# The first weights on a second DMA queue, and a shorter run of constant products, at the start of a gated hybrid block

## The chip, the cores and the metric

The kernel runs on one core of a Trainium2 chip. The metric is the device time of one execution in microseconds (us): 1506.85 is the median of 3 runs of the kernel before (1506.75 to 1508.6).

The core has five engines with a queue of instructions each: TensorE (PE: matrix products, with the weight loads shown apart as PEld), VectorE (DVE), ScalarE (ACT), GpSimd (POOL) and SyncE (SP). DMA transfers are issued by instructions on an engine's queue, here mostly SP's.

## The reference

The input x has 512 rows (frames) of 2048 channels. With a row norm ahead, it goes through one wide projection, whose columns feed a gated linear recurrence (branch A), a differential attention (branch B) and two merge gates; the branches are projected back, merged and projected out:

```
h    = x * rsqrt(mean(x^2) + eps) * norm_w
proj = h @ w_in                                  # 2048 -> 8*1024 + 2*2048
ya   = hgrn2(a_q, a_f, a_i) * silu(a_g)          # 8 heads of 128, chunks of 64
yb   = diff_attention(b_q, b_k, b_v) * silu(b_g) # 8 heads
out  = x + (sigmoid(gate_a) * (ya @ w_branch_a)
          + sigmoid(gate_b) * (yb @ w_branch_b)) @ w_out
```

The change touches only the start of the first piece of `h @ w_in`.

## The kernel before, in words

All activations are kept transposed, channels on the 128 partitions and the 512 frames along the row; x arrives as 16 tiles of 128x512 (`xT`). Products are made in a split form: each float32 operand is cut into a high part (rounded to the fp32r type) and a low part (the remainder), and high x high, high x low and low x high are summed in PSUM. So every tile of x and every tile of weights needs two conversions before TensorE can use it: a copy on ScalarE for the high part (L134 for x, L182 for weights) and a subtraction on VectorE for the low part (L135, L183).

`gemm` (L164 and on) runs over steps of KC = 2 tiles of 128 channels. In one step it loads the weights of both tiles (128x2x512, `raw`), converts them into `whi` and `wlo`, and issues 4 column blocks x 2 tiles x 3 products, 24 in all, into four PSUM accumulators. Three rings of buffers serve the weights: two raw ones, three high and three low. The conversions stand under a higher priority.

`proj_a(0, True)` is the first gemm: eight steps for the columns of q and f of the first two heads. Since nothing is loaded yet, its function `before` issues the loads of x tile by tile beside those of the weights, all on SP's queue, and calls `load_h`, which makes the high and low parts of x (L134, L135) and the running sum of squares (L138, L140, L141). The first step is converted tile by tile, the later ones as a whole. Its weights come in two pieces per tile, 128x256 each, one for the columns of q and one for those of f. The norm factor of each frame is applied after the product, so `make_rstd` (L143 and on) runs inside the last step.

Ahead of that stand a small load of constants on ScalarE's queue (L97), the tile `ones` (L101), one exponential on ScalarE that brings its table load (L105), and 14 products of `ones` with itself into a PSUM tile that is not read (L109). In the trace each of these float32 products is two passes, so 14 are 28.

The order of instructions on each engine is not the order of the text: the tile framework plans it (`schedule_with_timeline_sim=True`) from priorities, which follow the text, and a simulated timeline. Slots for x and for other 128x512 tiles (`slots`) are handed out first in, first out.

Further on come the other projections and mixers, the gates and the last projection by a scheme with seven half-size products (L677, with conversions L639, L640 and splits L577, L578); the change does not touch them.

Of the kernel before, what the change touches and what calls it, by code (L numbers as in the profile page):

```python
# [11 lines left out]
F32R = mybir.dt.float32r  # L12
# [5 lines left out]
P = 128  # L18
T = 512
NT = T // P  # L20
D = 2048
NK = D // P
WA = 1024
# [6 lines left out]
KC = 2  # L30
# [36 lines left out]
def hybrid_block(ctx: ExitStack, tc: tile.TileContext, xT, w_in, w_a, w_b, w_out,  # L67
                 smalls, cbase, cmask, outT):
    nc = tc.nc
# [14 lines left out]
    slots = Slots(spool, NSLOT)  # L84
    bigs = Slots(bpool, NBIG, "b", (P, 2, T))

    raws, his, los = deque((16, 17)), deque((18, 19, 20)), deque((21, 22, 23))

    def acc_tile():
        return ps_acc.tile([P, T], F32, name="acc", tag="acc")  # L90

    def mix_tile():
        return ps_mix.tile([P, T], F32, name="mix", tag="mix")


    sm = lead.tile([P, LEAD], F32, name="sm")
    nc.scalar.dma_start(out=sm[:, 0:C_LAM], in_=smalls[:, 0:C_LAM])  # L97
    ident = const.tile([P, P], F32, name="ident")
    make_identity(nc, ident)
    ones = const.tile([P, P], F32, name="ones")  # L100
# [4 lines left out]
    nc.scalar.activation(out=warm, in_=ones[:, 0:1], func=AF.Exp)  # L105

    ps0 = mix_tile()
    for i in range(14):
        nc.tensor.matmul(ps0[:, 0:P], lhsT=ones, rhs=ones, start=True, stop=True)  # L109
    masks_s = slots.get(U8, (P, 4, 384))  # L110
    masks = masks_s[0]
# [1 line left out]
    def load_masks():  # L113
        for i in range(4):
            mi = slots.get(mybir.dt.int32)
            nc.sync.dma_start(out=mi[0][:, 0:384], in_=cmask[:, i, :])
            nc.gpsimd.tensor_copy(out=masks[:, i, :], in_=mi[0][:, 0:384])
            slots.put(mi)
# [11 lines left out]
    def load_h(k, xs):  # L130
        sq = slots.get()
        x_t = xs[0]
        nw = sm[:, C_NW + k:C_NW + k + 1]
        nc.scalar.activation(out=h_hi[k], in_=x_t, func=AF.Copy, scale=nw)  # L134
        nc.vector.scalar_tensor_tensor(out=h_lo[k], in0=x_t, scalar=nw, in1=h_hi[k].bitcast(F32),  # L135
                                       op0=MUL, op1=SUB)
        if k == 0:
            nc.scalar.activation(out=xacc, in_=x_t, func=AF.Square)  # L138
        else:
            nc.scalar.activation(out=sq[0], in_=x_t, func=AF.Square)  # L140
            nc.vector.tensor_tensor(out=xacc, in0=xacc, in1=sq[0], op=ADD)  # L141
        slots.put(xs, sq)
# [21 lines left out]
    def gemm(wsrc, nk, a_hi, a_lo, stationary_w, evac, before=None, after=None, done=None, turn_at=1):  # L164
        accs = [acc_tile() for _ in range(4)]
        nb = nk // KC
        for kb in range(nb):
            if kb == turn_at:
                while later:
                    later.pop(0)()  # L170
            three = [bigs.get(ring=raws), bigs.get(F32R, ring=his), bigs.get(F32R, ring=los)]
            raw, whi, wlo = (t for t, _ in three)
            if before is not None:
                before(kb, wsrc(raw, kb))
            else:
                for dst, src in wsrc(raw, kb):
                    nc.sync.dma_start(out=dst, in_=src)
            with tc.high_priority(offset=PRIO):
                step = 1 if before is not None and kb == 0 else KC
                for c in range(0, KC, step):  # L180
                    cs = slice(c, c + step)
                    nc.scalar.activation(out=whi[:, cs, :], in_=raw[:, cs, :], func=AF.Copy)  # L182
                    nc.vector.tensor_tensor(out=wlo[:, cs, :], in0=raw[:, cs, :], in1=whi[:, cs, :].bitcast(F32),  # L183
                                            op=SUB)
            if after is not None and kb == nb - 1:
                with tc.high_priority(offset=PRIO):
                    after()
            for j in range(4):
                for c in range(KC):
                    k = kb * KC + c  # L190
                    js = slice(j * P, (j + 1) * P)
                    if stationary_w:
                        prods = ((whi[:, c, js], a_hi[k]), (whi[:, c, js], a_lo[k]), (wlo[:, c, js], a_hi[k]))
                    else:
                        prods = ((a_hi[k][:, js], whi[:, c, :]), (a_hi[k][:, js], wlo[:, c, :]),
                                 (a_lo[k][:, js], whi[:, c, :]))
                    for n, (l, r) in enumerate(prods):
                        nc.tensor.matmul(accs[j], lhsT=l, rhs=r, start=(k == 0 and n == 0),  # L198
                                         stop=(k == nk - 1 and n == 2))
                if kb == nb - 1:  # L200
                    with tc.high_priority(offset=PRIO):
                        evac(j, accs[j])
            for ring, (_, i) in zip((raws, his, los), three):
                ring.append(i)
            recent[:] = [whi[:, 0, :]]
            if done is not None:
                done(kb)
# [7 lines left out]
    def two_cols(w, c0, c1):  # L215
        def src(raw, kb):
            r = []
            for i, c in enumerate((c0, c1)):
                rows = w[kb * KC * P:(kb + 1) * KC * P, c:c + T // 2].rearrange("(c p) n -> p c n", p=P)
                r.append((raw[:, :, i * (T // 2):(i + 1) * (T // 2)], rows))  # L220
            return r
        return src


    def evac_rows(tiles):
        def evac(j, acc):
            s = slots.get()
            nc.scalar.activation(out=s[0], in_=acc, func=AF.Copy, scale=rstd_t[:, j:j + 1])
            tiles.append(s)
        return evac  # L230


    def evac_cols(tiles):
        def evac(j, acc):
            s = slots.get()
            nc.vector.tensor_tensor(out=s[0], in0=acc, in1=rstdB, op=MUL)
            tiles.append(s)
        return evac

    def silu(aps):  # L240
        n = aps[0].shape[1]
        sg = [slots.get() for _ in aps]
        for a, g in zip(aps, sg):
            nc.scalar.activation(out=g[0][:, 0:n], in_=a, func=AF.Sigmoid)
        for a, g in zip(aps, sg):
            nc.vector.tensor_tensor(out=a, in0=a, in1=g[0][:, 0:n], op=MUL)
        slots.put(*sg)
# [162 lines left out]
    def proj_a(p, first):  # L410
        c = p * 256
        qz, vg = [], []
        before = after = None
        if first:
            xs = [slots.get() for _ in range(NK)]

            def load_x(k):
                nc.sync.dma_start(out=xs[k][0], in_=xT[k * P:(k + 1) * P, :])

            def before(kb, wsrc):  # L420

                for k in range(3 * kb - 1, min(3 * kb + 2, NK)) if kb else ():
                    load_x(k)
                for c in range(KC):
                    k = kb * KC + c
                    if kb == 0:
                        load_x(c)
                    for dst, src in wsrc:
                        nc.sync.dma_start(out=dst[:, c], in_=src[:, c])
                    load_h(k, xs[k])  # L430
            after = make_rstd
        gemm(two_cols(w_in, c, WA + c), NK, h_hi, h_lo, True, evac_cols(qz), before, after)
        if first:
            load_masks()
        gemm(two_cols(w_in, 2 * WA + c, 3 * WA + c), NK, h_hi, h_lo, False, evac_rows(vg))
        silu([t[0] for t in qz[0:2]])
        sp = [slots.get(), slots.get()]
        for i in range(2):
            nc.scalar.activation(out=sp[i][0], in_=qz[2 + i][0], func=AF.Sigmoid)
            nc.scalar.activation(out=qz[2 + i][0], in_=qz[2 + i][0], func=AF.Sigmoid, scale=-1.0)  # L440
        silu([t[0][:, 256:512] for t in vg])
        return qz[0:2], sp, qz[2:4], vg
# [290 lines left out]
    def head_b(head, tiles):  # L733
        mix_b(head, tiles, bias, (1, head))
        slots.put(*tiles)

    st = proj_a(0, True)

    nc.sync.dma_start(out=sm[:, C_LAM:N_SMALL], in_=smalls[:, C_LAM:N_SMALL])
# [33 lines left out]
    for p in range(1, 4):  # L773
        mixers_a(p, proj_a(p, False))
# [311 lines left out]
```

## Time and profile before

| | |
|---|---|
| median of 3 runs | 1506.85 us |
| profiled execution: its time | 1507.68 us |
| profiled execution: its span, first to last instruction | 1505.9 us |
| TensorE busy | 1489.9 us, 99% of the span |
| VectorE busy | 1031.6 us, 69% |
| ScalarE busy | 718.7 us, 48% |
| mean granted TensorE clock | 0.999 |

All times inside the profile are counted from the start of the span. A busy TensorE is not TensorE at its peak: products overlap, and the same product takes longer at a lower clock. "Idle before" is the time in which the engine had nothing to do just before an instruction, with what ended it. DMA issues appear on the issuing engine's queue (SPq, ACTq), where they take time of that queue, and the time to landing is counted from the issue.

### The profile page before, as it was taken

How to read it: one execution, taken by the hardware profiler on the slowest of the kernel's cores; microseconds unless marked ns; L12 is line 12 of the kernel's file. 1: busy time of each engine (PE TensorE's matmuls, PEld its weight loads, DVE VectorE, ACT ScalarE, POOL GpSimd, SP SyncE). 2: the span in 40 equal slices, each digit the busy share in tenths (PEclk: the TensorE clock that was granted, in tenths of full speed). 3: DMA queues.
4: the chain of work that ended last, by engine and by line, in shares of the span. 5: the costliest groups of instructions: out<-in, count | busy, mean ns of one | idle time of the engine just before them, and what ended most of it. 6: DMA issues, size and time to landing. Idle time of an engine off the chain costs nothing.

```text
span 1505.9 us, 21697 instructions
## 1 busy us (share of the span) xinstructions
PE 1489.9 (99%) x7956; PEld 1284.5 (85%) x7956; DVE 1031.6 (69%) x2005; ACT 718.7 (48%) x1092; POOL 82.9 (6%) x94
## 2 busy tenths in 40 slices
PE   9999999999999999999999999999999999989999
PEld 8888888888888888888888888888888888879999
DVE  8656666575675547676755545888887776797875
ACT  7533643545435445564556443554444454343332
POOL 1000000001011101101110000000000000000000
PEclk9999999999999999999999999999999999999999
DMA  7332322322324346355549787554444466675440
GB/s 249 99 98 84 104 81 82 112 71 90 119 76 122 116 123 217 116 173 174 175 133 306 233 286 217 147 162 146 147 129 131 140 185 207 195 219 159 143 126 29
DMA packets 270874, 222.83 MB, mean 148 GB/s; under 512 B 13040, under 2 KB 230768, under 8 KB 270768
## 3 DMA queue, kind: packets, MB, share of 16 engines
q1 hardware_dynamic: 266704, 214.88, 46.0%
q10 hardware_dynamic: 3984, 6.31, 1.6%
q8 instruction: 62, 1.02, 0.3%
q14 instruction: 44, 0.36, 0.1%
q0 software_dynamic: 80, 0.26, 0.1%
HBM read 179.46 MB, written 35.65 MB: 143 GB/s over the span
## 4 chain that ended last, share of the span: by engine, by line
PE 94%; DVE 3%; DMA 2%; ACT 0%; issue 0%; ACTq 0%; SPq 0%; DVEq 0%
PE acc L198 55%; PE acc L677 26%; PE mix L677 4%; PE mix L317 3%; DMA s<-s 1%; PE mix L541 1%; DVE s L904 1%; PE mix L513 1%; PE mix L512 1%; PE mix L534 1%; DMA hs_d<-s 1%; DVE s L578 0%; PE mix L402 0%; PE mix L109 0%; PE mix L274 0%; DVE b L640 0%
## 5 line engine op out<-in xcount | busy, mean ns | idle before, releaser
L198 PE MATMUL acc<-b,b 128*128 128x512 f32 x3840 | 911.2, 393 | 0.0
L198 PEld LDWEIGHTS acc<-b,b 128*128 128x128 f32 x3840 | 713.2, 188 | 142.8 <-DVE b L183 0.4
L183 DVE TENSOR_TENSOR b<-b,b 128x1024 fp32r<-128x1024 f32 (+1 forms) x161 | 195.8, 1216 | 183.6 <-ACT b L182 169.0
L182 ACT ACTIVATE b<-b 128x1024 fp32r<-128x1024 f32 (+1 forms) x161 | 169.2, 1051 | 277.0 <-PE acc L198 216.3
L639 ACT ACTIVATE b<-b 128x1024 fp32r<-128x1024 f32 x168 | 175.8, 1059 | 262.8 <-PE acc L677 195.5
L677 PE MATMUL acc<-s,b 128*128 128x256 f32 (+1 forms) x1792 | 289.9, 316 | 8.3 <-DVE s L904 6.4
L677 PEld LDWEIGHTS acc<-s,b 128*128 128x128 f32 x1792 | 250.7, 190 | 36.1 <-DVE s L904 11.5
L640 DVE TENSOR_TENSOR b<-b,b 128x1024 fp32r<-128x1024 f32 x168 | 203.7, 1221 | 23.8 <-ACT b L639 22.6
L677 PE MATMUL acc<-b,b 128*128 128x256 f32 (+1 forms) x896 | 145.4, 317 | 0.6 <-DVE b L640 0.6
L677 PEld LDWEIGHTS acc<-b,b 128*128 128x128 f32 x896 | 126.8, 192 | 12.5 <-DVE b L640 0.8
L631 DVE TENSOR_TENSOR b<-b,b 128x1024 f32<-128x1024 f32 x96 | 117.3, 1221 | 0.7
L677 PE MATMUL mix<-s,b 128*128 128x512 f32 (+1 forms) x448 | 75.8, 315 | 1.8 <-DVE b L640 1.3
L677 PEld LDWEIGHTS mix<-s,b 128*128 128x128 f32 x448 | 64.4, 190 | 8.6 <-DVE b L640 1.5
L333 DVE COPY_PREDICATED s<-s,mix 128x128 f32<-128x128 uint8 (+3 forms) x176 | 52.0, 338 | 14.1 <-PE mix L317 13.0
L577 ACT ACTIVATE s<-s 128x256 fp32r<-128x256 f32 x96 | 37.1, 411 | 49.3 <-DVE s L951 23.1
L904 DVE TENSOR_TENSOR s<-s,acc 128x512 f32<-128x512 f32 x16 | 11.0, 688 | 56.1 <-PE acc L677 56.1
L518 ACT ACTIVATE s<-s,mn 128x128 f32<-128x128 f32 (+3 forms) x64 | 35.5, 555 | 23.8 <-DVE mn L515 23.7
L317 PE MATMUL mix<-qm,s 128*128 128x192 f32 x256 | 46.8, 326 | 0.0
L317 PEld LDWEIGHTS mix<-qm,s 128*128 128x128 f32 x256 | 42.7, 190 | 1.6
L461 POOL TENSOR_TENSOR qr<-qs,mhalf 128x4 f32<-128x4 f32 x32 | 35.5, 1116 | 115.6 <-DVE qs L460 115.6
L578 DVE TENSOR_TENSOR s<-s,s 128x256 fp32r<-128x256 f32 x96 | 38.3, 421 | 4.4 <-ACT s L577 3.9
L515 DVE CUSTOM_DVE_ANT_0 s<-mix,bias 128x128 f32<-128x128 f32 (+3 forms) x64 | 28.9, 487 | 13.5 <-PE mix L513 13.2
(159 smaller groups left out, 1114.5 us busy)
## 6 DMA issues: line engine op xcount, KB each, us to landing
b<-in_w_in_dram SPq DMA_DIRECT2D x240, 256.0 KB, 3.0
b<-in_w_in_dram SPq DMA_DIRECT2D x64, 512.0 KB, 4.1
b<-in_w_out_dram SPq DMA_DIRECT2D x32, 512.0 KB, 4.3
s<-in_xT_dram SPq DMA_DIRECT2D x46, 256.0 KB, 4.1
hs_d<-s SPq DMA_DIRECT2D x40, 256.0 KB, 3.7
y_d<-s SPq DMA_DIRECT2D x32, 256.0 KB, 2.8
b<-y_d SPq DMA_DIRECT2D x32, 256.0 KB, 4.7
b<-in_w_a_dram SPq DMA_DIRECT2D x32, 256.0 KB, 3.9
```

The source lines that it names most:

```text
L182: nc.scalar.activation(out=whi[:, cs, :], in_=raw[:, cs, :], func=AF.Copy)
L183: nc.vector.tensor_tensor(out=wlo[:, cs, :], in0=raw[:, cs, :], in1=whi[:, cs, :].bitcast(F32), op=SUB)
L198: nc.tensor.matmul(accs[j], lhsT=l, rhs=r, start=(k == 0 and n == 0), stop=(k == nk - 1 and n == 2))
L317: nc.tensor.matmul(ps[:, i * 192:(i + 1) * 192], lhsT=kt[:, tt * P:(tt + 1) * P], rhs=qm[:, tt * 192:(tt + 1) * 192], start=True, stop=True)
L333: nc.vector.copy_predicated(out=ov[:, :, a:b], mask=kv[:, :, s0:s0 + b - a], data=dv[:, :, s0:s0 + b - a])
L461: nc.gpsimd.tensor_tensor(out=rr, in0=ss, in1=mhalf[:, 0:4], op=ALU.pow)
L577: nc.scalar.activation(out=out[..., lh], in_=x, func=AF.Copy)
L578: tt(out=out[..., rh], in0=x, in1=out[..., lh].bitcast(F32), op=SUB)
L631: tt(out=r[x][0], in0=r[x][0], in1=r[y][0], op=ADD)
L639: nc.scalar.activation(out=xh[0], in_=x, func=AF.Copy)
L640: tt(out=xl[0], in0=x, in1=xh[0].bitcast(F32), op=SUB)
L677: nc.tensor.matmul(o, lhsT=l, rhs=r, start=(first and k == 0 and n == 0), stop=(k == NS - 1 and n == len(prods) - 1), skip_group_check=True)
```

## The change

The weights of the first step (two tiles, two pieces each) are issued by ScalarE's queue right behind the small load, each beside the load of the x tile, which stays on SP's queue. The raw buffer and the first two slots of x are therefore taken at the top. `before` no longer issues anything for step 0 and `gemm` uses the buffer already filled. The products of the constant tile go from 14 to 9.

```diff
     nc.scalar.dma_start(out=sm[:, 0:C_LAM], in_=smalls[:, 0:C_LAM])
+
+    raw0, xs = bigs.get(ring=raws), []
+    for c in range(KC):
+        xs.append(slots.get())
+        nc.sync.dma_start(out=xs[c][0], in_=xT[c * P:(c + 1) * P, :])
+        for i in range(2):
+            nc.scalar.dma_start(out=raw0[0][:, c, i * (T // 2):(i + 1) * (T // 2)],
+                                in_=w_in[c * P:(c + 1) * P, i * WA:i * WA + T // 2])
     ident = const.tile([P, P], F32, name="ident")
...
     ps0 = mix_tile()
-    for i in range(14):
+    for i in range(9):
         nc.tensor.matmul(ps0[:, 0:P], lhsT=ones, rhs=ones, start=True, stop=True)
...
-            three = [bigs.get(ring=raws), bigs.get(F32R, ring=his), bigs.get(F32R, ring=los)]
+            pre = before is not None and kb == 0
+            three = [raw0 if pre else bigs.get(ring=raws), bigs.get(F32R, ring=his), bigs.get(F32R, ring=los)]
...
-            xs = [slots.get() for _ in range(NK)]
+            xs.extend(slots.get() for _ in range(NK - KC))
...
-                    if kb == 0:
-                        load_x(c)
-                    for dst, src in wsrc:
-                        nc.sync.dma_start(out=dst[:, c], in_=src[:, c])
+                    if kb:
+                        for dst, src in wsrc:
+                            nc.sync.dma_start(out=dst[:, c], in_=src[:, c])
                     load_h(k, xs[k])
```

## Rows read from the trace of the kernel before

**Rows 1.** The page: busy us (share) xinstructions; the chain that ended last, by engine.
```profile
PE 1489.9 (99%) x7956; PEld 1284.5 (85%) x7956; DVE 1031.6 (69%) x2005; ACT 718.7 (48%) x1092; POOL 82.9 (6%) x94
...
PE 94%; DVE 3%; DMA 2%; ACT 0%; issue 0%; ACTq 0%; SPq 0%; DVEq 0%
```

**Rows 2.** The chain that ended last, from 0 to 60 us: start, us, what.
```profile
1.04 6.19 PE mix L109 x28
7.23 31.37 PE acc L198 x137
```

**Rows 3.** TensorE in order of time: start, us, engine, line, op, names, shapes, count.
```profile
6.99 0.71 PE L198 MATMUL acc<-b,b 128*128 128x512 f32 x2
...
39.24 6.20 PE L198 MATMUL acc<-b,b 128*128 128x512 f32 x26
45.28 1.05 PE L156 MATMUL mix<-s,ones 128*128 128x128 f32 x8
```

**Rows 4.** TensorE by groups, 4.0 to 4.5 and 7.0 to 7.25 us: busy us, mean ns.
```profile
L109 PE MATMUL mix<-ones 128*128 128x128 f32 x4 | 1.1, 421 | 0.0
...
L109 PE MATMUL mix<-ones 128*128 128x128 f32 x2 | 0.5, 324 | 0.0
```

**Rows 5.** SP's queue in order of time, 0 to 7.5 us.
```profile
0.72 0.39 SPq L418 DMA_DIRECT2D s<-in_xT_dram  x1
1.17 0.90 SPq L429 DMA_DIRECT2D b<-in_w_in_dram  x2
2.10 0.43 SPq L418 DMA_DIRECT2D s<-in_xT_dram  x1
2.58 0.91 SPq L429 DMA_DIRECT2D b<-in_w_in_dram  x2
```

**Rows 6.** ScalarE in order of time, 0 to 7.5 us.
```profile
0.72 0.41 ACTq L97 DMA_DIRECT2D sm<-in_smalls_dram  x1
1.17 1.28 ACT L105 ACT_TABLE_LOAD   x1 [1.17 <-PEq L1075]
2.46 0.20 ACT L105 ACTIVATE warm<-ones 128x1 f32<-128x1 f32 x1
3.45 0.63 ACT L138 ACTIVATE s<-s 128x512 f32<-128x512 f32 x1 [0.78 <-DMA s<-in_xT_dram]
3.98 0.71 ACT L134 ACTIVATE b<-s,sm 128x512 fp32r<-128x512 f32 x1
4.60 0.20 ACT L749 ACTIVATE ee<-ee 128x16 f32<-128x16 f32 x1
5.16 0.63 ACT L182 ACTIVATE b<-b 128x512 fp32r<-128x512 f32 x1 [0.36 <-DMA b<-in_w_in_dram]
```

**Rows 7.** DMA issues of 1.0-1.6, 1.6-2.09 and 2.09-2.5 us: KB, us to landing.
```profile
b<-in_w_in_dram SPq DMA_DIRECT2D x1, 128.0 KB, 2.7
...
b<-in_w_in_dram SPq DMA_DIRECT2D x1, 128.0 KB, 3.4
...
s<-in_xT_dram SPq DMA_DIRECT2D x1, 256.0 KB, 3.8
```

**Rows 8.** A stretch (PE, PEld, DVE, ACT, POOL busy, clock, DMA); one VectorE subtraction.
```profile
12.00:14.00 2.00, 2.00 (x11) 1.65 (x10) 2.00 (x4) 2.00 (x5) 0.00 (x0) 1.00 1.05 341
...
12.53 1.22 DVE L183 TENSOR_TENSOR b<-b,b 128x1024 fp32r<-128x1024 f32 x1
```

**Rows 9.** TensorE in order of time near 1350 us, with idle before and what ended it.
```profile
1349.28 1.17 PE L677 MATMUL acc<-s,b 128*128 128x256 f32 x5 [1.47 <-DVE s L578]
...
1351.42 0.93 PE L677 MATMUL acc<-b,b 128*128 128x256 f32 x4 [0.57 <-DVE b L640]
```

**Rows 10.** TensorE by stretches there: us, busy (starts), granted clock, DMA share, GB/s.
```profile
1352.00:1354.00 2.00, 2.00 (x11) 0.50 1.09 329
1354.00:1356.00 2.00, 2.00 (x14) 0.70 1.02 351
1356.00:1358.00 2.00, 2.00 (x19) 1.00 1.11 382
```

## The prediction

> **What bounds the kernel now.** I read the page first. TensorE is busy for 1489.9 of 1505.9 us and 94% of the chain that ended last is its own work [rows 1], so a change counts only by what it does to TensorE's start, pace or waits. The chain's opening comes next: nothing but the constant products (L109) from 1.04 to 7.23, then the real products (L198) without a break [rows 2]. The order of time on each engine shows what the first real product had to wait for [rows 3, 5, 6]: ScalarE had made the high part of the first weights (L182) by 5.16 + 0.63 = 5.79, and the normalised input by 3.98 + 0.71 = 4.69; the first real product stands at 6.99, behind the last constant product. So the constant products, not the data, set TensorE's real start today, by 1.2 us.
>
> How fast TensorE runs there matters too. The page's clock column reads full in the opening, but the pace says otherwise: 28 passes of 128x128 in 6.19 us are 0.221 us each, against at most 1.05 / 8 = 0.131 for the same shape at 45 us [rows 3], and a pass lasts 421 ns at 4 us and 324 at 7 us [rows 4]. I read the constant products as running at 1.2 GHz until about 7.0 and at 2.4 from there on, so that hardly a real product ran at the low level.
>
> **The constant products.** Five of 14 go, 10 of 28 passes: 18 x 0.221 = 3.98, so they end at 1.04 + 3.98 = 5.02 instead of 7.23. That is worth up to 1.2 us (to 5.79), if the data were as early as now.
>
> **ScalarE's queue.** It now issues the four weight pieces between its own small load and the table load. SP's pairs took 0.90 and 0.91 us [rows 5], so four cost 4 x 0.45 = 1.80 with their gaps. The table load moves from 1.17 to 2.97. Behind it stand, one after the other, from start to start in [rows 6]: table load 1.29, warm 0.20 (to 4.46), Square 0.53, high part of the input 0.62, the small exponential 0.20, then L182 from 5.81 to 6.44. Today the Square waits 0.78 for the input and L182 0.36 for weights; these waits vanish in the new lateness, so the 1.80 shows as 0.65. First real product: 6.5, which is 0.5 earlier than now. If the planner lets the Square and the exponential stand back, 4.46 + 0.62 + 0.63 = 5.7. If it issues the weights behind the table load and the warm-up instead, the second piece is issued near 3.1 and, with the 3.4 us that it takes to land [rows 7], lands at 6.5; L182 then ends at 7.2. I take 6.5, because L97, which is also a load issued first in the text, stands ahead of the table load now.
>
> The page "ScalarE: Activation LUTs" of the Trainium skill (What ACT_TABLE_LOAD costs) counts 2.66 us for a switch, 1.38 of it a drain. This case's rows show 1.28 and the next instruction 0.01 behind it; by the page the start would be 7.9 and the sum 1.4 higher. The row decides.
>
> **The weights' landing.** The first piece is issued at 1.17 as before; only the second step's pieces go out sooner, by 0.5 us, and the second input tile by 0.9. Landing took 2.7, 3.4 and 3.8 us for the first piece, the second and that tile [rows 7], so the first pair lands near 5.0, ahead of the 5.81 at which ScalarE would use it. I count nothing; ScalarE's own lateness hides it. If the two queues slow each other by less than 0.8 us it is still hidden.
>
> **SP's queue.** It is rid of four issues and of everything behind them: the next step's inputs leave 1.8 us sooner. ScalarE and VectorE are full from 12 to 14 us and beyond [rows 8], so they can't use it. Nothing.
>
> **The later conversions.** ScalarE's chain is 0.65 late, and being full it stays late: the low part of the second step's weights ends at 12.53 + 1.22 = 13.75 now [rows 8] and at 14.4 then. Its first use today, in the written order, would be at 6.99 + 26 x 0.238 = 13.2 (26 products in 6.20 us [rows 3]), and yet TensorE did not stop: the order has cover of at least 0.6. With TensorE slower in the opening (next term) the demand comes later too. I take nothing, and 0.7 as the upper end.
>
> **The clock.** This is the term that decides. Between 5.02 and 6.5 TensorE now has a hole of 1.5 us, after 4.0 us of constant products instead of 6.2, and at that point the level has not yet risen. The only place where the trace shows such a thing is late in the kernel: behind holes of 1.47 and 0.57 us [rows 9] the granted clock stands at 0.50, and it is back near 1355.2 (a mean of 0.70 over 1354 to 1356), 3.8 us after the product at 1351.42 that ended the second hole. The products' count is 11 in 2 us at the low level and 19 at the high one [rows 10], so a low stretch loses 8/19 = 0.42 of itself. Taken over to the opening, as an estimate: real products at 1.2 GHz from 6.5 to 10.3, 0.42 x 3.8 = 1.6 us lost. Bounds: the level rises near 7.0 as it does today, 0.2 lost; or the low stretch behind the hole is as long as today's, from 1.04 to 7.0, so 5.9 us, and 2.5 are lost. I take 1.6, from the row with a hole in it.
>
> **Sum.** -0.5 for the start, +1.6 for the clock, nothing for the rest: +1.1. The profiled execution took 1507.68 (span 1505.9), so 1508.8; the median of the runs shown is 0.83 lower, so **1508.0**. About 0.2% (3.0 us) is what can be told from no change, and this is inside it. The forecast's own range runs from -1.3 (start 5.7, clock risen) to +2.7 (start 7.2, 2.5 lost): 1505.5 to 1509.6.
>
> **Rival 1: the hole does no harm.** The level rises during the constant products or as soon as the first real ones run, and the start is 5.7 to 6.5: -0.5 to -1.3, some 1506.0. For it: the gap is only 1.5 us, and at 1347.8 it took two holes close together. Against it: today the level had not risen after 4 us of constant products [rows 4]. Also the low parts could then come too late by up to 0.7, which would eat the gain. The page "TensorE: Matmul & The Clock Gate" of the Trainium skill (Part 1) says that the throttled level is the default, released by activity, and that the same kernel shows different numbers of slow products from run to run; by that this rival and the forecast can both occur, in different runs of one kernel. No row here shows two runs.
>
> **Rival 2, the slower side: the planner writes another order further on.** The orders of all engines come from a simulated timeline, in which the opening moves. The dear place is 1347 to 1355 us, where TensorE follows VectorE: one more pair of such holes (1.47 + 0.57 [rows 9]) and one more low stretch (1.6) are 3.6 us, with the forecast's 1.1 together 1511.6. It decides once a conversion there stands one place later on VectorE. Against it: from about 40 us TensorE paces everything, so a shift of the opening moves all alike.
>
> **Rival 3: the same, to the good.** The holes and the low stretch at 1350 go: -3.6, with a start gained of 0.5 some 1502.8.
>
> **Chances.** Forecast 0.53, rival 1 0.24, rival 2 0.13, rival 3 0.10. The forecast's upper end reaches past the 3.0 us only with all bounds together (0.02). So faster 0.10, same 0.75, slower 0.15. The range takes in the forecast's own and rival 1's, and reaches a little towards the other two: 1504.2 to 1510.6.
>
> **What would show it.** The table load near 3.0 and L182 at 5.8; 18 passes of L109 ending near 5.0; an idle of TensorE of about 1.5 us; the first L198 near 6.5; products some 0.43 us apart instead of 0.23 until about 10. At 30 us the count of L198 should stand some 4 to 5 behind that of now. The forecast is wrong if the products are at full pace from the start, if weights are issued behind the table load, if the first product waits for a DMA, or if the waits between 1338 and 1352 are not those of now.

## The result, and the profile after

The changed kernel takes 1519.12 us (median of 4 runs, 1517.42 to 1520.15) against 1506.8 us for the kernel before on the same chip (median of 4, 1506.19 to 1508.6): 12.3 us more, a ratio of 1.0079 with a 95% interval of 1.0061 to 1.0096. The forecast was 1508.0 in a range of 1504.2 to 1510.6; the time is 8.5 us above its upper end. The profiled execution took 1517.42 us, with a span of 1515.6.

The page of the kernel after: busy us (share) by engine, and the chain by engine.

```profile
PE 1489.6 (98%) x7946; PEld 1283.3 (85%) x7946; DVE 1031.3 (68%) x2005; ACT 718.4 (47%) x1092; POOL 82.1 (5%) x94
...
PE 93%; DVE 3%; DMA 3%; ACT 1%; issue 0%; SPq 0%; ACTq 0%; DVEq 0%
```

TensorE is as busy as before to 0.3 us [rows 1], in a span 9.7 us longer: on balance the time is waits. (Inside the busy time, the low stretches found below are offset by ten passes of the constant product fewer, 2.0 us, and by a low stretch near 1352 us that this execution did not have, 1.4.) TensorE in order of time, kernel after, 0 to 46 us (start, us, line, names, shapes, count, idle before and what ended it):

```profile
1.04 4.21 PE L117 MATMUL mix<-ones 128*128 128x128 f32 x18 [1.04 <-DVE mhalf L111]
9.10 4.41 PE L207 MATMUL acc<-b,b 128*128 128x512 f32 x12 [3.86 <-ACT b L142]
14.78 8.46 PE L207 MATMUL acc<-b,b 128*128 128x512 f32 x36 [1.27 <-ACT b L191]
29.14 8.89 PE L207 MATMUL acc<-b,b 128*128 128x512 f32 x31 [5.91 <-ACT b L191]
```

The real products (L207, L198 before) start at 9.10 instead of 6.99 [rows 3] and then stop twice, for 1.27 and 5.91 us, for a conversion of weights on ScalarE (L191, L182 before). Before, they ran from the start without a break [rows 2]. 12 products a tile and 24 a step: the first stop is for the second tile of step one, the second for step three. ScalarE in the same stretch shows why:

```profile
1.17 2.72 ACTq L104 DMA_DIRECT2D b<-in_w_in_dram  x4
6.42 1.28 ACT L191 ACT_TABLE_LOAD   x1 [6.42 <-DMA b<-in_w_in_dram]
7.71 0.63 ACT L191 ACTIVATE b<-b 128x512 fp32r<-128x512 f32 x1
8.25 0.19 ACT L113 ACTIVATE warm<-ones 128x1 f32<-128x1 f32 x1
8.34 0.71 ACT L142 ACTIVATE b<-s,sm 128x512 fp32r<-128x512 f32 x1
...
14.11 1.56 ACT L191 ACTIVATE b<-b 128x512 fp32r<-128x512 f32 x2
...
28.05 1.99 ACT L191 ACTIVATE b<-b 128x1024 fp32r<-128x1024 f32 x2
```

Two things differ from [rows 6]. The first conversion now stands ahead of the warm-up exponential, and with it the table load: the table load waits for the weights until 6.42. And the further conversions stand later among the work on x: the second tile's at 14.11 behind five tiles of x (before: behind two), the third step's at 28.05 behind all sixteen (before: behind eight, at 15.39). ScalarE is not idle in between; it works through x first, at 1.13 us a tile. SP's queue has another order too:

```profile
4.46 2.35 SPq L437 DMA_DIRECT2D b<-in_w_in_dram  x4
7.37 6.24 SPq L427 DMA_DIRECT2D s<-in_xT_dram  x11
14.07 2.32 SPq L124 DMA_DIRECT2D s<-in_cmask_dram  x4
16.72 4.23 SPq L437 DMA_DIRECT2D b<-in_w_in_dram  x8
```

There are two raw buffers, so the third step's weights need the first step's buffer. It is free when the second tile's low part is made, on VectorE from 15.46 to 16.11. So SP, in the planned order, issues eleven tiles of x and the four masks first and the third step's weights from 16.72 on. In the kernel before they left at 9.06, in this row of SP's queue:

```profile
9.06 1.75 SPq L429 DMA_DIRECT2D b<-in_w_in_dram  x4
```

This late load is not what TensorE waited for, though. The kernel after, issues of 16.6 to 18.9 us (KB, median us to landing):

```profile
b<-in_w_in_dram SPq DMA_DIRECT2D x4, 128.0 KB, 3.8
```

By this the third step's weights had landed by about 22.5, and the row of its conversion at 28.05 shows no wait: it stood behind the work on x on ScalarE.

The holes also lower the clock. TensorE by stretches, kernel after (busy, products, granted clock, DMA share, GB/s; the count, called starts in [rows 10], takes in products under way at a stretch's edges):

```profile
8.00:10.00 2.00, 0.90 (x2) 0.67 1.03 289
10.00:12.00 2.00, 2.00 (x6) 0.50 0.87 264
...
28.00:30.00 2.00, 0.86 (x2) 0.50 0.00 0
30.00:32.00 2.00, 2.00 (x6) 0.50 0.00 0
32.00:34.00 2.00, 2.00 (x9) 0.86 0.39 110
```

A mean of 0.67 over 8 to 10 us is the high level until about 8.7: TensorE had idled since 5.25 when the clock fell. Products run at 1.2 GHz from 9.1 to about 12.1 and from 29.1 to about 32.6; at the prediction's 0.42 lost of such a stretch that is 1.3 and 1.5. The sum: start 2.1, waits 1.3 and 5.9, low stretches 2.8, together 12.1. VectorE reads the first results of this gemm from their accumulators 12.6 us apart, in the kernel before and in the kernel after:

```profile
49.53 1.40 DVE L236 TENSOR_TENSOR s<-acc,rstdB 128x512 f32<-128x512 f32 x2
```

```profile
62.12 1.40 DVE L245 TENSOR_TENSOR s<-acc,rstdB 128x512 f32<-128x512 f32 x2
```

All of the loss is thus made by the end of the first gemm, at 62 us. The spans differ by less, 9.7. One reason is the low stretch near 1352 [rows 10]: the profiled execution before has it, and that of after, behind a hole of the same 0.57 us, has not. TensorE there, before and after:

```profile
1351.42 3.71 PE L677 MATMUL acc<-b,b 128*128 128x256 f32 x17 [0.57 <-DVE b L640]
```

```profile
1362.66 2.29 PE L685 MATMUL acc<-b,b 128*128 128x256 f32 x17 [0.57 <-DVE b L648]
```

That is 1.4 us. These products start 11.2 apart, so another 1.3 was won back between 62 and 1362 us; where is not shown.

### The profile page after: what moved, and what is told of

The parts are those of the page before. It is cut to its first block, busy times and chain, and to the rows that moved or that the text cites. A ratio compares the mean times of both kernels' runs of the same rounds, so it can differ in the third digit from the quotient of the medians.

```text
span 1515.6 us, 21679 instructions
## 1 busy us (share of the span) xinstructions
PE 1489.6 (98%) x7946; PEld 1283.3 (85%) x7946; DVE 1031.3 (68%) x2005; ACT 718.4 (47%) x1092; POOL 82.1 (5%) x94
## 4 chain that ended last, share of the span: by engine, by line
PE 93%; DVE 3%; DMA 3%; ACT 1%; issue 0%; SPq 0%; ACTq 0%; DVEq 0%
PE acc L207 54%; PE acc L685 26%; PE mix L685 4%; PE mix L326 3%; PE mix L549 1%; DMA s<-in_xT_dram 1%; DVE s L912 1%; PE mix L520 1%; PE mix L521 1%; PE mix L542 1%; PE mix L411 0%; DVE s L586 0%; PE mix L283 0%; PE mix L484 0%; DVE b L648 0%; DMA sm<-in_smalls_dram 0%
## 5 line engine op out<-in xcount | busy, mean ns | idle before, releaser
L207 PE MATMUL acc<-b,b 128*128 128x512 f32 x3840 | 914.5, 394 | 11.0 <-ACT b L191 7.2
L207 PEld LDWEIGHTS acc<-b,b 128*128 128x128 f32 x3840 | 715.4, 189 | 155.3 <-ACT b L191 8.0
L191 ACT ACTIVATE b<-b 128x1024 fp32r<-128x1024 f32 (+1 forms) x161 | 169.0, 1051 | 284.5 <-PE acc L207 218.2
L237 ACT ACTIVATE s<-acc,rstd_t 128x512 f32<-128x512 f32 x48 | 32.5, 678 | 10.9 <-PE mix L549 7.7
```

## The experiments

Theories. **Order**: issuing the first weights from ScalarE's queue makes the planner write another order on ScalarE and SP, and that order is the loss. **Clock**: the hole behind the shorter run of constant products is. **Landing**: the weights come late because two queues share the DMA engines. Each run was compared with the kernel before on one chip.

**e1, nine products alone.**

```diff
-    for i in range(14):
+    for i in range(9):
```

> The kernel before with 9 constant products instead of 14 and nothing else. Order theory (the planner's new order on ScalarE makes the loss): the order on ScalarE is the old one, so real products start when the first weights are converted, near 5.8, or at the clock's pace a little later; 1505.5 to 1508.5. Clock theory (the hole behind the shorter run keeps TensorE at 1.2 GHz and that starts the loss): 1509 or more, with real products some 0.43 us apart until 10 us or longer.

1505.43 us, ratio 0.9998 (0.9989 to 1.0007). Nine products alone do no harm that can be told. The forecast's clock term is there all the same. TensorE up to 14 us in the kernel before:

```profile
6.99 7.32 PE L198 MATMUL acc<-b,b 128*128 128x512 f32 x31
```

The same in e1, up to 14 us, and a stretch of it:

```profile
6.26 7.91 PE L198 MATMUL acc<-b,b 128*128 128x512 f32 x27 [1.01 <-ACT b L182]
...
8.00:10.00 2.00, 2.00 (x7) 1.00 1.06 383
```

Real products start 0.73 earlier, run at half pace at first (7 in 2 us) and are 4 fewer by 14 us. In this execution the gain of the start and the loss of the pace nearly cancel.

**e2, the changed kernel with 14 products.**

```diff
-    for i in range(9):
+    for i in range(14):
```

> The changed kernel with all 14 constant products back. Order theory: the first real product still stands near 9.1, TensorE still waits about 1.3 and 5.9 us for ScalarE's conversions, only the first low stretch shrinks: 1517 to 1519.5. Clock theory: the time comes back to 1507 to 1510.

1518.44, ratio 1.009 (1.0075 to 1.0105). The clock theory falls; the number of products does not matter here. (The first low stretch did not shrink as expected: the first product came later, at 9.7, and the low clock behind it lasted until 13.4.)

**e3, table load first.** `issue_after` keeps what stands in its block behind the named instruction on that engine.

```diff
-    nc.scalar.activation(out=warm, in_=ones[:, 0:1], func=AF.Exp)
+    warm_ins = nc.scalar.activation(out=warm, in_=ones[:, 0:1], func=AF.Exp)
...
-                    nc.scalar.activation(out=whi[:, cs, :], in_=raw[:, cs, :], func=AF.Copy)
+                    with tc.issue_after(warm_ins.ins):
+                        nc.scalar.activation(out=whi[:, cs, :], in_=raw[:, cs, :], func=AF.Copy)
```

> The changed kernel with one edge in the order: the first conversion of weights is kept behind the warm-up exponential, so the table load no longer stands behind the wait for the weights. Order theory: ScalarE starts the conversion when the weights land, near 6.4 instead of 7.7, first real product near 7.7; the later waits stay and TensorE reaches them earlier, so most of the 1.3 us is lost again in the wait for the third step's conversion, which the work on x on ScalarE paces: that conversion comes up to 1.3 us sooner, 1517.5 to 1519. Landing theory (the weights come late because two queues share the DMA engines): no change from 1519 by more than 1.5 us either; the two are told apart by the next run.

1518.45, ratio 1.0084 (1.0068 to 1.0101). ScalarE, and TensorE's waits up to 46 us (total, times, longest):

```profile
3.88 1.28 ACT L113 ACT_TABLE_LOAD   x1 [3.88 <-DMA s<-in_xT_dram]
5.18 0.20 ACT L113 ACTIVATE warm<-ones 128x1 f32<-128x1 f32 x1
7.86 0.63 ACT L192 ACTIVATE b<-b 128x512 fp32r<-128x512 f32 x1 [2.48 <-DMA b<-in_w_in_dram]
...
PE acc L208 <- ACT b L192: 6.1, 2, 5.9
```

The table load is out of the way, but in this execution the weights landed at 7.86 instead of 6.42, so the conversion is no sooner, and the wait of 5.9 for the third step stays. The time was inside what I expected, but the start was not: 9.16, not 7.7.

**e4, the conversions among the work on x.**

```diff
+                    ins = nc.scalar.activation(out=whi[:, cs, :], in_=raw[:, cs, :], func=AF.Copy)
+                    conv.append(ins.ins)
...
+                    if kb:
+                        with tc.issue_after(conv[kb // 2 + 1 if kb > 2 else 1]):
+                            load_h(k, xs[k])
...
```

The conversion that a step's work on x is kept behind is one to four steps earlier, by the index.

> The changed kernel with the other part of the order put back: the work on x of each step stays behind a conversion of weights two steps earlier, as in the kernel before; the table load still stands behind the wait for the weights. Order theory: the wait of 5.9 us near 23 to 29 us goes, with it the low stretch behind it (1.6 us) and most of the wait of 1.3; what stays is the start at 9.1 (2.1 us late) and the first low stretch (1.4): 1508.5 to 1512. Landing theory or clock theory: within 1.5 us of 1519.

1509.87, ratio 1.003 (1.0018 to 1.0042). Nothing but an order was changed, and 9 of the 12 us are back. TensorE's waits up to 46 us and the table load:

```profile
PE acc L208 <- ACT b L142: 5.0, 1, 5.0
...
7.53 1.28 ACT L191 ACT_TABLE_LOAD   x1 [7.53 <-DMA b<-in_w_in_dram]
```

One wait is left, the late start: at 10.2, since the weights landed at 7.53 and the table load stood behind them.

**e5, both.** The edits of e3 and e4 together.

> Both parts of ScalarE's order put back in the changed kernel (table load ahead of the wait for weights; work on x behind a conversion two steps earlier); weights still on ScalarE's queue, 9 products. Order theory alone: no wait is left that the kernel before did not have, first real product near 6.5 to 7.7: 1506 to 1508. Order and landing theory (the first weights land 1.3 to 2.7 us later because the second queue shares the DMA engines with the loads that SP issues meanwhile): first conversion not before 6.4 to 7.9, first real product near 8 to 9, half the pace for some us behind it: 1508 to 1510.

1507.17, ratio 1.0007 (0.9998 to 1.0016). With the order put back, the change makes no difference that can be told. That the first weights landed late shows here too:

```profile
1.17 2.77 ACTq L104 DMA_DIRECT2D b<-in_w_in_dram  x4
3.97 1.28 ACT L113 ACT_TABLE_LOAD   x1 [3.97 <-DMA s<-in_xT_dram]
...
5.85 0.63 ACT L192 ACTIVATE b<-b 128x512 fp32r<-128x512 f32 x1 [0.38 <-DMA b<-in_w_in_dram]
...
7.14 33.21 PE L209 MATMUL acc<-b,b 128*128 128x512 f32 x138 [2.12 <-ACT b L142]
```

Four issues took 2.77 us, because the last waits for a transfer of x (the release that the table load's row names), not 1.80. This is the order that the forecast's sum described: start 7.1 against 6.5 there, and 1.0007 against the 1.0008 of 1508.0 over 1506.85. The interval takes in no change as well, so the agreement does not confirm the terms of the sum.

**e6, the same place in the text, SP's queue.**

```diff
-            nc.scalar.dma_start(out=raw0[0][:, c, i * (T // 2):(i + 1) * (T // 2)],
+            nc.sync.dma_start(out=raw0[0][:, c, i * (T // 2):(i + 1) * (T // 2)],
```

> The changed kernel with its new place in the text and its 9 products, but the first weights issued by SP's queue. Order theory: it is the issue from ScalarE's queue, not the place in the text, that makes the planner move the conversions; the order on ScalarE is the old one, no wait of several us, first real product near 6.3: 1505 to 1507.5, as the kernel before with 9 products. If the place in the text were the cause: 1515 to 1520.

1505.27, ratio 0.9993 (0.9983 to 1.0003). The place in the text is innocent; ScalarE's queue is what tips the order.

**e7, one tile by ScalarE's queue.**

```diff
-            nc.scalar.dma_start(out=raw0[0][:, c, i * (T // 2):(i + 1) * (T // 2)],
+            (nc.scalar if c == 0 else nc.sync).dma_start(out=raw0[0][:, c, i * (T // 2):(i + 1) * (T // 2)],
```

> Only the first tile's two pieces go by ScalarE's queue, the second tile's by SP's; 9 products. The planner here puts the table load first and the two conversions together behind the work on the first two x tiles. Order theory: no wait of several us, 1506 to 1509. Landing theory: first piece pair lands after 5.0 all the same. If any issue from ScalarE's queue were enough to bring the loss: above 1515.

1506.88, ratio 1.0004 (0.9995 to 1.0013). Two issues of 128 KB do no harm: the third step's conversion stands behind eight tiles of x, and the only wait for ScalarE is the start's:

```profile
PE acc L207 <- ACT b L191: 1.6, 1, 1.6
```

**e8, SP held back.** e5, and SP's loads behind a transfer of 8 bytes that reads the first tile's weights.

```diff
+    spare = dram.tile([1, 2], F32, name="spare")
+    gate = nc.sync.dma_start(out=spare, in_=raw0[0][0:1, 0, T - 2:T])
...
+                with tc.issue_after(gate.ins):
                     nc.sync.dma_start(out=xs[k][0], in_=xT[k * P:(k + 1) * P, :])
```

> The run with both parts of the order put back, and besides SP's further loads (x tiles from the third on, the second step's weights, masks) wait until the first tile's weights have landed; added is a transfer of 8 bytes as the gate. Landing theory by shared DMA engines: the first pair lands near 4.5 to 5.0 instead of 6.4 to 7.9 and the first real product stands near 6.2 to 6.8; what follows comes later by some us (the second step's data), so the time tells little: 1506 to 1510. If ScalarE's queue is slow by itself: landing stays at 6.4 or later.

1506.23, ratio 1.0001 (0.9992 to 1.001). The first conversion starts at 5.69, behind two pieces of work on x. The gate, which needs the weights, leaves SP at the same time:

```profile
5.69 0.63 ACT L195 ACTIVATE b<-b 128x512 fp32r<-128x512 f32 x1
...
5.69 0.31 SPq L107 DMA_DIRECT2D spare<-b  x1
```

The second piece of the first tile, issued by ScalarE's queue near 1.65, in e8 and then in e5 (KB, us to landing):

```profile
b<-in_w_in_dram ACTq DMA_DIRECT2D x1, 128.0 KB, 4.0
...
b<-in_w_in_dram ACTq DMA_DIRECT2D x1, 128.0 KB, 4.1
```

In after, e2, e4 and e3 it took 4.7 to 6.1. Neither expectation came: the weights landed neither by 5.0 nor at 6.4 or later. Without the gate ScalarE or its table load could start on them at 5.85, 6.42, 7.03, 7.53 and 7.86 (e5, after, e2, e4, e3, issued at the same times). So with SP held back they come at the early end of that spread, hardly ahead of e5, and later than in the kernel before, where the same piece took 3.4 [rows 7]. Whether shared engines make the rest is not shown; nor does one profiled execution each show how much of the spread belongs to the kernels.

**e9, the small load on SP's queue.**

```diff
-    nc.scalar.dma_start(out=sm[:, 0:C_LAM], in_=smalls[:, 0:C_LAM])
+    nc.sync.dma_start(out=sm[:, 0:C_LAM], in_=smalls[:, 0:C_LAM])
```

> The changed kernel with the small load of constants moved to SP's queue, so that the fourth weight piece on ScalarE's queue has no transfer to wait for. The planner still puts the first conversion ahead of the table load, but the work on 12 tiles of x stands ahead of the third step's conversion instead of 16 (8 in the kernel before). Order theory, by dose: that conversion comes 4 x 1.13 = 4.5 us sooner, so of the wait of 5.9 us some 1.4 stay and the low stretch behind it shrinks or goes: 1511 to 1515, between the two kernels. If only the late start counted: 1518 to 1520.

1511.45, ratio 1.0038 (1.0025 to 1.0052), between the two kernels as expected by dose.

**e10, one transfer per tile**, and **e11, three pieces by ScalarE's queue**:

```diff
-        for i in range(2):
-            nc.scalar.dma_start(out=raw0[0][:, c, i * (T // 2):(i + 1) * (T // 2)],
-                                in_=w_in[c * P:(c + 1) * P, i * WA:i * WA + T // 2])
+        nc.scalar.dma_start(out=raw0[0][:, c, :].rearrange("p (s n) -> p s n", s=2),
+                            in_=w_in[c * P:(c + 1) * P, 0:2 * WA].rearrange("p (s n) -> p s n", s=2)[:, :, 0:T // 2])
```

```diff
-            nc.scalar.dma_start(out=raw0[0][:, c, i * (T // 2):(i + 1) * (T // 2)],
+            (nc.sync if c and i else nc.scalar).dma_start(out=raw0[0][:, c, i * (T // 2):(i + 1) * (T // 2)],
```

> The changed kernel with one transfer per tile (256 KB) instead of two on ScalarE's queue, the same bytes. The planner then puts the table load first and the conversions among the work on x as in the kernel before (third step behind 8 tiles). Order theory: what sets the planner off is the time that ScalarE's queue spends on the issues, not the bytes on it: 1505.5 to 1508. Landing theory as the main cause: the same bytes by the same queue, 1515 or more.

> The changed kernel with three of the four pieces on ScalarE's queue and the last on SP's. The planner puts the table load first; the conversions stand among the work on x nearly as before. Order theory: 1505.5 to 1508.5, so the fourth issue is what tips the order. If the loss grew with each issue on ScalarE's queue: some 1512 to 1516.

1511.47, ratio 1.0038 (1.0024 to 1.0052), and 1510.11, ratio 1.0026 (1.0017 to 1.0036). Both are misses: the second step's conversion stands as before, but the third step's stands behind 13 and 12 tiles of x, not eight. The third step's conversion, then TensorE's waits for conversions up to 46 us, in e9, e10 and e11:

```profile
22.42 1.05 ACT L191 ACTIVATE b<-b 128x1024 fp32r<-128x1024 f32 x1
...
PE acc L207 <- ACT b L191: 2.7, 1, 2.7
```

```profile
21.46 1.04 ACT L190 ACTIVATE b<-b 128x1024 fp32r<-128x1024 f32 x1
...
PE acc L206 <- ACT b L190: 4.7, 2, 3.1
```

```profile
19.84 1.04 ACT L191 ACTIVATE b<-b 128x1024 fp32r<-128x1024 f32 x1
...
PE acc L207 <- ACT b L191: 4.5, 2, 2.8
```

Put together, with the tiles of x that stand ahead of the third step's conversion on ScalarE, its start, the first real product and the ratio:

| kernel | x tiles ahead | starts at | first product | ratio |
|---|---|---|---|---|
| before | 8 | 15.4 | 7.0 | 1 |
| e1, e6, e7, e8, e5 | 8 | 14.9 to 17.4 | 6.0 to 7.1 | 0.9993 to 1.0007 |
| e4 | 8 | 20.1 | 10.2 | 1.003 |
| e11 | 12 | 19.8 | 7.0 | 1.0026 |
| e9 | 12 | 22.4 | 8.0 | 1.0038 |
| e10 | 13 | 21.5 | 6.8 | 1.0038 |
| after, e2, e3 | 16 | 28.1 to 28.7 | 9.1 to 9.7 | 1.0079 to 1.009 |

The loss goes with the order, not with the bytes on the queue: e5 sends the same 512 KB by ScalarE's queue as the changed kernel, and with the order put back no loss can be told. Nor is it the table load alone: that stands first in e3, e10 and e11. Where it stands behind the weights and the other conversions are in place (e4), the late start is what is left of the loss.

What tips the planner is less clear. In e7 and e10 ScalarE's queue has two issues, which take as long:

```profile
1.17 0.93 ACTq L104 DMA_DIRECT2D b<-in_w_in_dram  x2
```

```profile
1.18 0.97 ACTq L103 DMA_DIRECT2D b<-in_w_in_dram  x2
```

Yet only e10, with 512 KB against 256, gets the worse order. So the time of the issues, which I had named for e10, is not what tips it alone. With two, three and four pieces of 128 KB by ScalarE's queue (e7, e11, after) the loss grows, 1.0004, 1.0026 and 1.0079, as e11's other expectation had it in kind (in size it said 1512 or more), and the tiles of x ahead grow with it: 8, 12 and 16.

**e12, a candidate:** e6 with 12 constant products.

```diff
-    for i in range(9):
+    for i in range(12):
```

> A candidate: first weights and x tiles issued at the top of the text, all on SP's queue, 12 constant products, so that they end near 6.4, close to the first conversion's end. Clock theory for the small rest: without a hole the clock rises with the constant products, real products from 6.4 at full pace: 0.3 to 0.8 us under the kernel before, 1505 to 1506, hardly to be told from it.

1505.45, ratio 0.9996 (0.9987 to 1.0005). As fast as the kernel before; no version beats it by what can be measured. The constant products did not end near 6.4 but at 5.35, since 24 passes took hardly longer than the 18 of the changed kernel:

```profile
1.04 4.31 PE L117 MATMUL mix<-ones 128*128 128x128 f32 x24 [1.04 <-DVE mhalf L111]
```

**The clock across the runs.** With the same 18 passes ahead, real products behind a hole of TensorE did not always run at half pace. The stretch from 8 to 10 us in e7, then in e8 and e11 (the clock column reads 1.00 in each, the products' count differs):

```profile
8.00:10.00 2.00, 2.00 (x7) 1.00 1.07 258
...
8.00:10.00 2.00, 2.00 (x10) 1.00 1.01 360
...
8.00:10.00 2.00, 2.00 (x10) 1.00 1.01 314
```

The holes before the first real product are 1.55, 1.12 and 1.70 us; e1, at half pace too, had 1.01. So the length of the hole does not tell the two apart: in some of the profiled executions the clock had risen by then, in others not. The low stretch near 1352 us comes and goes as well: over 1335 to 1370 us the mean granted clock is 1.00 in after, e2, e5 and e7 and 0.95 in the other ten profiles. Each kernel has one profile; what its other executions did is not recorded.

## Why the prediction was wrong

**The step that failed** is the order on ScalarE. The prediction took the first product at 6.5 "because L97, which is also a load issued first in the text, stands ahead of the table load now", and for the later conversions it said "I take nothing, and 0.7 as the upper end". Both assume that the conversions keep their places. The planner moved them: 2.1 us at the start, 7.2 of waits, 2.8 of low clock, where the sum had -0.5, nothing and 1.6. e4 and e5, which put back nothing but places, take the ratio from 1.0079 to 1.003 and 1.0007.

**The constant products**: right, 18 passes from 1.04 to 5.25 against 5.02.

**ScalarE's queue**: wrong in size too. Four issues took 2.72, not 1.80, with a wait in the last one that I had not named.

**The weights' landing**: I counted nothing, taking the first pair to land near 5.0 and ScalarE's lateness to hide it. In the changed kernel the table load, standing behind the weights, started only at 6.42, so the landing is part of the late start; in e3 ScalarE waited 2.48 for it. It is small beside the order: with that put back (e5) the start is 7.1.

**SP's queue**: "Nothing" holds for the data that came earlier, but the order of SP changed as well, and with two raw buffers the second tile's late conversion made the third step's load late. That load landed 5 us or more ahead of its conversion, so it is not what was paid for.

**The clock**: right in e1, with half pace behind the hole until about 10 us and 4 products fewer by 14 us. (The profile's clock column reads 1.00 there; the count of products told it.) But the term that "decides" was taken from one execution, and it is not fixed: e8 and e11 ran at full pace behind holes of 1.12 and 1.70, which is what rival 1 said, and the changed kernel ran at full pace behind the very holes near 1350 that the 3.8 us came from. In its opening the clock had risen and fell again, behind longer holes than the forecast's. The 0.42 is low, since the counts of [rows 10] take in products at the edges: in e3, 12 products at the low level took 5.49 us and 36 at the high one 8.48, so a low stretch loses nearly half of itself:

```profile
9.16 5.49 PE L208 MATMUL acc<-b,b 128*128 128x512 f32 x12 [4.12 <-ACT b L142]
14.83 8.48 PE L208 MATMUL acc<-b,b 128*128 128x512 f32 x36 [0.18 <-ACT b L192]
```

**Rival 2** named the mechanism, another order by the planner, but put it at 1347 us and gave it 0.13. Its argument against itself, that TensorE paces everything from about 40 us, was sound (of 12.6 us, 11.2 still stood 1300 us later) and pointed at the opening: there ScalarE is full [rows 8] and its order decides.

**Open**: why the planner's timeline puts the conversions so late when more than the first tile's weights go by ScalarE's queue (the runs show when it does, not how it reckons); how far the landing varies from one execution to another; and what decides whether the clock has risen when the real products start.

## What to carry to other kernels

A load moved to the queue of an engine that computes is an edit of that engine's order: where a planner writes the orders, read the new ones to the end of the stretch in which the engine is full before a price is set. Where the opening is bound by one engine's queue, its order can be worth more than an earlier issue: here 12.3 us against the 0.5 that the forecast hoped for. A low stretch that one profile shows is no price yet: look whether another execution has it behind the same hole.

## What the hardware showed that I had not expected

Behind 18 passes of constant products and a hole of 1.01 us, TensorE stayed at half pace to about 10 us (e1); behind the same 18 passes and a hole of 1.70 it ran at full pace (e11). Behind the same two holes near 1350 us, of 1.47 and 0.57, 17 products took 3.71 us before and 2.29 after. The first weights, landing by a second queue beside loads of x on the first, could be used at 5.85 to 7.86 us over five profiled executions, against 5.16 for the kernel before [rows 6].
